# Zero matmuls ahead of the first data, a first product in written order, a two-instruction root step and larger stores in a two-layer decoder trunk

## The chip, the cores and the metric

The kernel runs on one core of a Trainium2 chip. The metric is device time in microseconds, from the first to the last of the program as the device counts it; the median of three runs is 2240.84 (2240.35 to 2241.23). The profile is one execution, taken apart from those runs.

## What is computed

A trunk of two layers on 256 tokens of 2048 features, all in float32. Each layer adds a mixer and then a squared-ReLU MLP to the residual x, each behind an RMS norm, and a last RMS norm ends it:

```python
for layer in range(DEPTH):
    j = layer // 2
    h = rmsnorm(x, ln_mix[layer])
    if layer % 2 == 0:
        x = x + even_mixer(h, e_w_in[j], e_g_q[j], e_g_kv[j], e_w_uq[j], e_w_ukv[j], e_w_out[j], rope128, rope64)
    else:
        x = x + odd_mixer(h, o_w_in[j], o_w_out[j], rope128)
    h = rmsnorm(x, ln_mlp[layer])
    x = x + squared_relu_mlp(h, mlp_w1[layer], mlp_w2[layer])
return rmsnorm(x, ln_final)
```

Only two places of this matter here: the first 512 columns of `h @ e_w_in` (the queries' latent of the even mixer), and the last norm.

## The kernel before

**Tiles.** 256 tokens are two tiles of 128 (t = 0, 1), 2048 features are sixteen blocks of 128 (k = 0 to 15). Every operand of a large product is split into a high and a low half (`xh`, `xl` for the activations, both in the tile `xx`; `wh`, `wl` for the weights), so that one product is three matmuls: high by high (L170), high by low (L171), low by high (L172). Weights come from memory into one of three `raw` buffers by the queue of SP (L150); ACT makes the high half (a cast, L162), DVE subtracts it for the low half (L163).

**The first product.** `even_mixer` (L500) starts with `TokenGemm` on 512 columns of the weights: sixteen rows of weights, six matmuls of 512 columns for each. `step(i)` does rows 2i and 2i+1, `rows` any number. The activations are made on the way: `scaled_transpose` (L260) turns two blocks of features on PE (four transposes into one PSUM tile `pt`, L236), then for each block ACT copies it times its gain into `xh` (L270) and DVE makes `xl` (L271). `norm_block(..., late=True)` gives these as parts [0] and [1] and, as part [2], the squares of both tiles of tokens over 512 columns on ACT (`sumsq`, L258). The gains themselves are rows of 128 that are loaded and turned on PE (`load_gains`, L488): `pg` of 32 columns for ln_mix, later one of 38 for ln_mlp, e_g_q and e_g_kv.

**What sets the order.** The kernel is written in the order of its data; the framework's scheduler then reorders each engine's instructions by its own estimate, here too, and places the waits. On the chip every engine takes its own list in the order in which it stands. The queue of SP issues x in blocks of columns (`load_x`, L97), the identity (`cst`, L100), the rows of gains (L494) and the weights.

**The end.** The last MLP's `down` does its last 256 columns one tile of tokens after the other and calls `leave(t, cs)` (L809) for each: the sum of squares of the last columns (L813), `inverse_root` (L245: a guess from the exponent's bits at L249 and L250, then three Newton steps of three DVE instructions, L252 to L254), five pieces of the row scaled by the root on DVE and ACT in turn (L817 to L821), and four stores of 512 columns on SP's queue (L823).

Of the kernel before, what the change touches and what calls it, by code (L numbers as in the profile page):

```python
# [12 lines left out]
F32 = mybir.dt.float32  # L13
# [7 lines left out]
P = 128  # L21
# [19 lines left out]
def shape_constants():  # L41
    """Identity, rotary tables, and additive masks: functions of the shapes alone. Row p is token p of
    either tile, in cosT and sinT feature p; the first tile's queries see 128 keys, the second's 256."""

    def rope(dim):
        inv = (10000.0 ** (-np.arange(0, dim, 2, dtype=np.float32) / np.float32(dim)).astype(np.float64)).astype(np.float32)
        ang = (np.arange(S, dtype=np.float32)[:, None] * inv[None, :]).astype(np.float64)
        c, s = np.cos(ang).astype(np.float32), np.sin(ang).astype(np.float32)
        return c, s

    q = np.arange(S)[:, None]
    k = np.arange(S)[None, :]
# [15 lines left out]
def decoder_trunk(ctx, tc, const, x_in, ln_mix, ln_mlp, ln_final, e_w_in, e_g_q, e_g_kv, e_w_uq, e_w_ukv, e_w_out,  # L68
# [29 lines left out]

    load_x(0, 256)
    nc.sync.dma_start(ident, const[:, :P])  # L100
    # the activation table is loaded while the first data is on its way
    warm = small.tile([P, 1], F32, name="warm")
    nc.vector.memset(warm, 0.0)
    nc.scalar.activation(warm, warm, AF.Exp)

# [13 lines left out]
    # Slots whose readers may still be pending: taking one runs what frees it.  # L119
# [12 lines left out]
    class Weights:  # L132
        """Rows of 128 of the columns in srcs: four at a time (or as in loads) from memory, two at a time split."""
# [10 lines left out]
        def load(self):  # L144
            at, n = self.loads.popleft()
            raw = self.flat("raw", F32, n, 3, 2048)
            c = 0
            for s in self.srcs:
                w = s.shape[-1]
                nc.sync.dma_start(raw[:, :, c : c + w], s[at * P : (at + n) * P, :].rearrange("(k p) n -> p k n", p=P))  # L150
                c += w
            self.raw.append((at, n, raw))
# [23 lines left out]
    def bank(shape=(P, 512), wide=False):  # L176
        """A bank to accumulate in; wide: the scores' banks too."""
        if wide and next(turns) % 6 >= 4:
            return psc.tile(list(shape), F32, name=nm("acc"), tag="ps")
        return acc.tile(list(shape), F32, name=nm("acc"), tag="acc")  # L180

    class TokenGemm:
        """Tokens on partitions: o[t] is [P, width] for each tile of tokens. srcs: weights' columns."""
# [11 lines left out]
        def rows(self, k0, n):  # L195
            ah, al = self.act
            wh, wl = self.w.get(k0, n)
# [41 lines left out]
    def rsqrt(y, ss, n, mean_over):  # L239
        """y = (ss / mean_over + EPS) ** -0.5 on [P, n]."""  # L240
# [4 lines left out]
    def inverse_root(y, v, n):  # L245
        """v ** -0.5: a guess from the exponent's bits, Newton steps."""
# [13 lines left out]
    def scaled_transpose(src, gain, dst_h, dst_l):  # L260
        """dst[f, k, tok] = src[tok, k, f] * gain[f, k], in halves; src(t, k) is [P tokens, P features]. A list of parts."""
# [14 lines left out]
    def norm_block(i, n, ss, late=False):  # L276
        """Columns of the residual that are final: x.T * gain, as parts, and their part of the sum of squares."""
# [22 lines left out]
    def rope(dst, src, nh, hd, t, r):  # L300
        """dst, src: [P, nh * hd]; src times the row's r, rotated."""
# [29 lines left out]
    def heads(pool, src, tab, rate=1):  # L331
        """Four heads of 128 features of x, rotated, features on partitions: [P, 4, S]."""
# [24 lines left out]
    def attend(pool, scores, bias, scale, values, oh, ol, o0, done):  # L357
        """scores(h, out, t) fills [P, keys]; values(h, t): [P, HD]. Head h goes to oh/ol[:, o0 + h, :]."""
# [51 lines left out]
    def plain_transpose(tok, dst, done=None):  # L410
        """tok: a tile of rows for each tile of tokens; dst(k0, n, PSUM) stores n tiles of features. A list of parts."""
# [18 lines left out]
    def rotated(pool, o, hd, r, width=512):  # L430
        """Rotates [P, width] of both tiles of tokens."""
# [7 lines left out]
    def split_rows(pool, o, hd, r):  # L439
        """Rotates [P, 512] of both tiles and, later, puts features on partitions: [P, 4, S] in halves."""  # L440
# [24 lines left out]
    def project_out(oT, w, ss, i):  # L465
        """The first two blocks of columns begin while the last heads are pending."""
# [21 lines left out]
    def load_gains(at, gs):  # L488
        """Gains by feature: rows of 128, turned on the tensor engine."""
# [9 lines left out]

    def even_mixer(ss):  # L500
        w = e_w_in[0]
        with ExitStack() as st:
# [5 lines left out]
            # queries' and keys' latents, with the first norm on the way  # L508
            g = TokenGemm(act, KT, [w[:, 0:512]], loads=[(0, 1), (1, 1), (2, 2)] + [(k, 4) for k in range(4, KT, 4)])
            parts = [norm_block(0, n, ss, True) for n in range(4)]  # L510
            g.w.load()
            load_gains(0, [ln_mix])
            load_x(256, 512)
            parts[0][0]()
            g.rows(0, 1)
            g.w.load()
            parts[0][1]()
            g.rows(1, 1)
            load_x(512, 1024)
            g.w.load()  # L520
            parts[1][0]()
            g.step(1)
            parts[1][1]()
            load_x(1024, 1536)
            g.step(2)
            parts[0][2]()
            parts[2][0]()
            g.step(3)
            parts[2][1]()
            load_x(1536, 2048)  # L530
            g.step(4)
            parts[3][0]()
            load_gains(2 * KT, [ln_mlp, e_g_q, e_g_kv])
            nc.sync.dma_start(cst[:, P:], const[:, P:])
            g.step(5)
            parts[3][1]()
            for n in range(1, 4):
                parts[n][2]()
            g.step(6)
            g.step(7)  # L540
# [17 lines left out]
            # c_kv, k_pe, k_idx, w_idx; the two single keys padded for either head of a pair  # L558
# [24 lines left out]
            # index scores and the keys that they choose, as parts  # L583
# [135 lines left out]
    def mlp(layer, ss, done, tail=None):  # L719
        w1, w2 = mlp_w1[layer], mlp_w2[layer]  # L720
        NCH = 4
        with ExitStack() as st:
# [6 lines left out]
            def up(c):  # L729
                """Hidden features on partitions: relu(x @ w1) ** 2, transposed, of 2048 features."""  # L730
# [19 lines left out]
            def down(c, h):  # L750
# [10 lines left out]
                if last and tail:  # L761
                    # the last columns: one tile of tokens after the other, so that the first ends under the second
# [38 lines left out]
    def both(n, cs):  # L801
# [3 lines left out]
        if n == 3:  # L805
            nc.vector.tensor_reduce(pre, ss3, axis=AX.X, op=ALU.add)
            nc.vector.tensor_scalar(pre, pre, 1.0 / D, EPS, op0=ALU.mult, op1=ALU.add)

    def leave(t, cs):  # L809
# [3 lines left out]
        nc.vector.tensor_tensor_reduce(junk[:, : cs.stop - cs.start], x[:, t, cs], x[:, t, cs], 1.0 / D, pre[:, t : t + 1],  # L813
                                       op0=ALU.mult, op1=ALU.add, accum_out=v)
        inverse_root(r, v, 1)
        xt = x[:, t, :]
        nc.vector.tensor_scalar_mul(xt[:, :512], xt[:, :512], r)  # L817
        nc.scalar.activation(xt[:, 512:1024], xt[:, 512:1024], AF.Copy, scale=r)
# [3 lines left out]
        for h in range(0, D, 512):  # L822
            nc.sync.dma_start(ov[t][:, h : h + 512], xt[:, h : h + 512])  # L823
# [29 lines left out]
```

## Time and profile before

| | |
|---|---|
| median of the runs | 2240.84 us |
| span of the profiled execution | 2239.9 us |
| PE busy | 2224.8 us, 99% of the span |
| DVE busy | 1318.0 us, 59% |
| ACT busy | 1036.4 us, 46% |
| moved by DMA | 406.65 MB, mean 182 GB/s |

The span runs from the first to the last instruction of the profiled execution, and it is the time that sums are made against; the median of the runs lies 0.9 us above it. PE's busy time is made of overlapping pieces: a matmul's row ends with its last result, and the next has begun before that, so the pace of a row of matmuls is the distance of their starts, not the length of one. In the chain of waits that overlap is already taken off.

### The profile page before, as it was taken

How to read it: one execution, taken by the hardware profiler on the slowest of the kernel's cores; microseconds unless marked ns; L12 is line 12 of the kernel's file. 1: busy time of each engine (PE TensorE's matmuls, PEld its weight loads, DVE VectorE, ACT ScalarE, POOL GpSimd, SP SyncE). 2: the span in 40 equal slices, each digit the busy share in tenths (PEclk: the TensorE clock that was granted, in tenths of full speed). 3: DMA queues.
4: the chain of work that ended last, by engine and by line, in shares of the span. 5: the costliest groups of instructions: out<-in, count | busy, mean ns of one | idle time of the engine just before them, and what ended most of it. 6: DMA issues, size and time to landing. Idle time of an engine off the chain costs nothing.

```text
span 2239.9 us, 29663 instructions
## 1 busy us (share of the span) xinstructions
PE 2224.8 (99%) x12126; PEld 1913.7 (85%) x12126; DVE 1318.0 (59%) x1771; ACT 1036.4 (46%) x1369; POOL 0.2 (0%) x4
## 2 busy tenths in 40 slices
PE   8999999999999999999999999999999999999998
PEld 7899988888888888888899999888888888888887
DVE  6767665565545545655575666556565555465555
ACT  5444545555434434534444443455454344344333
POOL 0000000000000000000000000000000000000000
PEclk9999999999999999999999999999999999999999
DMA  7554545555555555555555555556555555555553
GB/s 244 177 164 148 170 137 172 183 187 187 188 188 189 188 188 190 188 188 186 188 171 170 177 164 170 173 180 204 190 181 192 189 191 188 188 187 190 188 188 132
DMA packets 207605, 406.65 MB, mean 182 GB/s; under 512 B 8614, under 2 KB 15468, under 8 KB 207340
## 3 DMA queue, kind: packets, MB, share of 16 engines
q1 hardware_dynamic: 207468, 404.75, 55.5%
q8 instruction: 95, 1.56, 0.3%
q14 instruction: 42, 0.34, 0.0%
HBM read 402.62 MB, written 2.10 MB: 181 GB/s over the span
## 4 chain that ended last, share of the span: by engine, by line
PE 99%; DMA 0%; DVE 0%; ACT 0%; SPq 0%; issue 0%; DVEq 0%
PE acc L226 21%; PE acc L172 21%; PE acc L171 21%; PE acc L170 21%; PE acc L227 11%; PE pt L236 1%; PE ps L458 1%; PE po L391 1%; PE pp L236 0%; PE po L392 0%; DMA raw<-in_e_w_in_dram 0%; PE ps L689 0%; PE ps L688 0%; DMA raw<-in_mlp_w_dram 0%; PE pi L170 0%; PE pi L171 0%
## 5 line engine op out<-in xcount | busy, mean ns | idle before, releaser
L163 DVE TENSOR_TENSOR wl<-raw,wh 128x1024 fp32r<-128x1024 f32 (+3 forms) x765 | 927.6, 1213 | 849.0 <-ACT wh L162 843.1
L162 ACT CAST wh<-raw 128x1024 fp32r<-128x1024 f32 (+3 forms) x765 | 794.5, 1039 | 1081.3 <-PE acc L172 572.1
L226 PE MATMUL acc<-xx,wh 128*128 128x512 f32 x2048 | 703.6, 395 | 0.0
L227 PE MATMUL acc<-xx,wl 128*128 128x256 f32 x2048 | 544.1, 281 | 0.0
L226 PEld LDWEIGHTS acc<-xx,wh 128*128 128x128 f32 x2048 | 378.2, 188 | 77.9
L172 PE MATMUL acc<-wh,hl 128*128 128x512 f32 (+1 forms) x1024 | 402.2, 393 | 0.0
L171 PE MATMUL acc<-wl,hh 128*128 128x512 f32 (+1 forms) x1024 | 400.0, 391 | 0.0
L227 PEld LDWEIGHTS acc<-xx,wl 128*128 128x128 f32 x2048 | 385.5, 188 | 12.5
L170 PE MATMUL acc<-wh,hh 128*128 128x512 f32 (+1 forms) x1024 | 361.0, 391 | 0.0
L171 PEld LDWEIGHTS acc<-wl,hh 128*128 128x128 f32 x1024 | 192.2, 188 | 45.8
L170 PEld LDWEIGHTS acc<-wh,hh 128*128 128x128 f32 x1024 | 191.7, 188 | 45.2
L172 PEld LDWEIGHTS acc<-wh,hl 128*128 128x128 f32 x1024 | 192.3, 188 | 44.2
L171 PE MATMUL acc<-xx,wh 128*128 128x256 f32 x768 | 216.5, 282 | 0.0
L170 PE MATMUL acc<-xx,wh 128*128 128x256 f32 x768 | 216.4, 282 | 0.0
L172 PE MATMUL acc<-xx,wl 128*128 128x256 f32 x768 | 215.5, 282 | 0.0
L171 PEld LDWEIGHTS acc<-xx,wh 128*128 128x128 f32 x768 | 144.7, 188 | 0.4
L170 PEld LDWEIGHTS acc<-xx,wh 128*128 128x128 f32 x768 | 144.7, 188 | 0.4
L172 PEld LDWEIGHTS acc<-xx,wl 128*128 128x128 f32 x768 | 144.3, 188 | 0.0
L171 PE MATMUL acc<-wl,xx 128*128 128x512 f32 (+1 forms) x320 | 127.5, 399 | 0.0
L172 PE MATMUL acc<-wh,xx 128*128 128x512 f32 (+1 forms) x320 | 125.5, 393 | 0.0
L170 PE MATMUL acc<-wh,xx 128*128 128x512 f32 (+1 forms) x320 | 119.7, 400 | 0.5 <-ACT xx L270 0.5
L171 PE MATMUL acc<-wl,oh 128*128 128x512 f32 x256 | 102.2, 399 | 0.0
(166 smaller groups left out, 1615.8 us busy)
## 6 DMA issues: line engine op xcount, KB each, us to landing
raw<-in_mlp_w_dram SPq DMA_DIRECT2D x252, 1024.0 KB, 5.1
raw<-in_o_w_in_dram SPq DMA_DIRECT2D x48, 1024.0 KB, 5.1
raw<-in_e_w_in_dram SPq DMA_DIRECT2D x35, 1024.0 KB, 5.1
raw<-in_e_w_out_dram SPq DMA_DIRECT2D x16, 1024.0 KB, 5.0
raw<-in_o_w_out_dram SPq DMA_DIRECT2D x16, 1024.0 KB, 5.1
raw<-in_mlp_w_dram SPq DMA_DIRECT2D x8, 512.0 KB, 3.8
raw<-in_e_w_uq_dram SPq DMA_DIRECT2D x4, 768.0 KB, 4.4
raw<-in_e_w_in_dram SPq DMA_DIRECT2D x4, 640.0 KB, 4.1
```

Of the source, the lines that this page charges most:

```text
L162: nc.scalar.copy(hi, raw)
L163: nc.vector.tensor_tensor(lo, raw, hi.bitcast(F32), op=ALU.subtract)
L170: nc.tensor.matmul(o, ah, bh, start=first, stop=False, **kw)
L171: nc.tensor.matmul(o, ah, bl, start=False, stop=False, **kw)
L172: nc.tensor.matmul(o, al, bh, start=False, stop=last, **kw)
L226: nc.tensor.matmul(self.o[f], wh[:, kk, fs], xx[:, k], start=k == 0, stop=False, skip_group_check=True)
L227: nc.tensor.matmul(self.o[f][:, 0, :], wl[:, kk, fs], xx[:, k, 0], start=False, stop=k == KT - 1, skip_group_check=True)
L236: nc.tensor.transpose(o, src, ident[: src.shape[0], : src.shape[0]])
L391: nc.tensor.matmul(po[0][:, h % 2, :], values(h, 0), pr[h][:, :S], start=True, stop=False)
L458: nc.tensor.matmul(o, q[:, h, t * P : t * P + P], k[:, h, : SPAN[t][1]], start=True, stop=True)
```

## The change

Four things are changed.

- **Ahead of the data.** A tile of zeros is set on DVE, and PE does seven matmuls of 512 columns on it before anything else. The identity and the rows of ln_mix (now a tile of their own, `rows0`) are loaded through ACT's queue.
- **The first product.** It moves into a new function, `first_product`, in a block in which the scheduler keeps the written order. The loads of x and weights stand together at its beginning; the first four rows of weights share one buffer and come in four loads; rows 0 to 3 are multiplied one at a time; the high half of row 0 is made on DVE. The loads of the second group of gains and of the remaining constants are issued after it.
- **The root.** `leave` no longer calls `inverse_root`; it halves its argument and does a Newton step in two DVE instructions instead of three.
- **The stores.** Each tile of tokens leaves in two stores of 1024 columns; the last one of the second tile is issued by ACT.

```diff
     load_x(0, 256)
-    nc.sync.dma_start(ident, const[:, :P])
+    nc.scalar.dma_start(ident, const[:, :P])
+    rows0 = cpool.tile([2 * KT, P], F32, name="rows0")
+    nc.scalar.dma_start(rows0, ln_mix.rearrange("l (k p) -> (l k) p", p=P))
+    zeros = wpool.tile([P, 512], F32R, name="zeros", tag="ra", bufs=1)
+    nc.vector.memset(zeros.bitcast(F32), 0.0)
     warm = small.tile([P, 1], F32, name="warm")
...
+    pw = psc.tile([P, 512], F32, name="pw", tag="ps")
+    for i in range(7):
+        nc.tensor.matmul(pw, zeros[:, :P], zeros, start=True, stop=True)
...
+    def first_product(g, w, parts):
+        raw = g.w.load(((0, 1), (1, 1)))
+        load_x(256, 512)
+        g.w.load(((2, 1), (3, 1)), raw)
+        load_x(512, 1024)
+        g.w.load(((4, 2), (6, 2)))
+        load_x(1024, 1536)
+        g.w.load(((8, 4),))
+        load_x(1536, 2048)
+        pg = psc.tile([P, 512], F32, name="pg", tag="ps")
+        pt = ptr.tile([P, 2, S], F32, name="pt0", tag="pt")
+        transposed(pg[:, : 2 * KT], rows0)
...
+        for a, b, k0 in ((xh, wh, True), (xl, wh, False), (xh, wl, False)):
+            for t in range(NT):
+                nc.tensor.matmul(g.o[t], a[:, 0, t * P : t * P + P], b, start=k0, stop=False)
+        parts[0][1]()
+        g.product(1, 1, *wts[1])
+        g.rows(2, 1)
+        parts[1][0]()
+        g.rows(3, 1)
+        parts[1][1]()
+        parts[0][2]()
+        g.step(2)
+        g.w.load(((12, 4),))
+        parts[2][0]()
+        parts[1][2]()
+        g.step(3)
+        parts[2][1]()
+        g.step(4)
+        parts[3][0]()
+        parts[2][2]()
+        g.step(5)
+        parts[3][1]()
+        parts[3][2]()
+        g.step(6)
+        g.step(7)
...
+            g = TokenGemm(act, KT, [w[:, 0:512]])
             parts = [norm_block(0, n, ss, True) for n in range(4)]
+            with tc.manual_schedule():
+                first_product(g, w, parts)
             load_gains(2 * KT, [ln_mlp, e_g_q, e_g_kv])
             nc.sync.dma_start(cst[:, P:], const[:, P:])
...
-        inverse_root(r, v, 1)
+        for _ in range(3):
+            nc.vector.scalar_tensor_tensor(b.bitcast(F32), r, v, r, op0=ALU.mult, op1=ALU.mult)
+            nc.vector.scalar_tensor_tensor(r, b.bitcast(F32), 1.5, r, op0=ALU.subtract, op1=ALU.mult)
         xt = x[:, t, :]
-        nc.vector.tensor_scalar_mul(xt[:, :512], xt[:, :512], r)
-        nc.scalar.activation(xt[:, 512:1024], xt[:, 512:1024], AF.Copy, scale=r)
+        nc.scalar.activation(xt[:, :512], xt[:, :512], AF.Copy, scale=r)
+        nc.vector.tensor_scalar_mul(xt[:, 512:1024], xt[:, 512:1024], r)
+        nc.sync.dma_start(ov[t][:, :1024], xt[:, :1024])
...
-        for h in range(0, D, 512):
-            nc.sync.dma_start(ov[t][:, h : h + 512], xt[:, h : h + 512])
+        (nc.scalar if t else nc.sync).dma_start(ov[t][:, 1024:], xt[:, 1024:])
```

What the block of written order makes of the engines' lists is not in these lines, so the place that decides follows, on two engines. A row is the line, the operation, what it writes and reads with buffer numbers, and the shape.

ACT before, in the middle of the first product. `wh_150` is the high half of rows 2 and 3, `wh_178` of 4 and 5, `wh_207` of 6 and 7; `pt_141` and `pt_166` hold the transposed features 4 to 7; `junk` rows are squares.

```order
L162 CAST wh_150<-raw_139 128x1024
L258 ACTIVATE junk_297,ss_82<-x 128x512
L270 ACTIVATE xx<-pt_141,gains 128x256
L270 ACTIVATE xx<-pt_166,gains 128x256
L258 ACTIVATE junk_299,ss_82<-x 128x512
L270 ACTIVATE xx<-pt_141,gains 128x256
L270 ACTIVATE xx<-pt_166,gains 128x256
L162 CAST wh_178<-raw_176 128x1024
L162 CAST wh_207<-raw_176 128x1024
L258 ACTIVATE junk_301,ss_82<-x 128x512
```

ACT after, about the same place. `wh_178` is now row 3, `wh_201` rows 4 and 5, `wh_232` rows 6 and 7; `pt_169` holds features 4 and 5, `pt_188` 6 and 7, `pt_219` 8 and 9.

```order
L284 ACTIVATE xx<-pt_169,gains 128x256 x2
L174 CAST wh_178<-raw_104 128x512
L284 ACTIVATE xx<-pt_188,gains 128x256 x2
L272 ACTIVATE junk_197,ss_94<-x 128x512
L272 ACTIVATE junk_199,ss_94<-x 128x512
L174 CAST wh_201<-raw_111 128x1024
L284 ACTIVATE xx<-pt_219,gains 128x256 x2
L272 ACTIVATE junk_228,ss_94<-x 128x512
L272 ACTIVATE junk_230,ss_94<-x 128x512
L174 CAST wh_232<-raw_111 128x1024
```

The casts, which stood two in a row, now stand singly, each behind two copies out of a fresh `pt` tile and, from `wh_201` on, two squares (but for one).

PE before, the transposes of features 4 to 7 and the first matmuls on rows 2 and 3.

```order
L236 MATMUL pt_141<-cst,x 128x128 x4
L236 MATMUL pt_166<-cst,x 128x128 x4
L170 MATMUL acc_88<-wh_150,xx 128x512
L170 MATMUL acc_89<-wh_150,xx 128x512
L171 MATMUL acc_88<-wl_151,xx 128x512
L172 MATMUL acc_88<-wh_150,xx 128x512
L171 MATMUL acc_89<-wl_151,xx 128x512
```

PE after, from the transposes of features 4 and 5 to the first matmuls on rows 4 and 5. `pg_352` is the turn of the second group of gains.

```order
L250 MATMUL pt_169<-cst,x 128x128 x4
L250 MATMUL pg_352<-cst,rows_348 128x38
L182 MATMUL acc_100<-wh_178,xx 128x512
L183 MATMUL acc_100<-wl_179,xx 128x512
L184 MATMUL acc_100<-wh_178,xx 128x512
L182 MATMUL acc_101<-wh_178,xx 128x512
L183 MATMUL acc_101<-wl_179,xx 128x512
L184 MATMUL acc_101<-wh_178,xx 128x512
L250 MATMUL pt_188<-cst,x 128x128 x4
L182 MATMUL acc_100<-wh_201,xx 128x512
L183 MATMUL acc_100<-wl_202,xx 128x512
```

Two blocks were turned in one go ahead of two steps; now one block is turned ahead of each step, and the turn of the gains stands ahead of row 3. The same alternation of four transposes and one step goes on to step 6.

## Rows read from the trace of the kernel before

**Rows 1.** The page: the chain that ended last, by engine.
```profile
PE 99%; DMA 0%; DVE 0%; ACT 0%; SPq 0%; issue 0%; DVEq 0%
```

**Rows 2.** Stretches: length, busy time per engine, PEclk, DMA share, GB/s.
```profile
0.00:15.00 15.00, 9.33 (x29) 7.03 (x30) 4.55 (x9) 8.95 (x20) 0.20 (x4) 1.00 0.83 275
15.00:37.00 22.00, 22.00 (x103) 17.53 (x102) 16.43 (x37) 13.93 (x26) 0.00 (x0) 1.00 0.74 251
...
100.00:2215.00 2115.00, 2115.00 (x11564) 1819.52 (x11563) 1236.17 (x1580) 975.64 (x1266) 0.00 (x0) 1.00 0.55 180
```

**Rows 3.** Waits of PE, 0 to 50 us: total, times, longest.
```profile
PE pt L236 <- DMA cst<-in_const_dram: 3.9, 1, 3.9
PE pt L236 <- DMA x<-in_x_dram: 1.2, 1, 1.2
PE acc L170 <- ACT xx L270: 0.5, 1, 0.5
```

**Rows 4.** Chain of waits, 12 to 26 us: start, us, what.
```profile
12.82 0.85 PE acc L172 x2
...
20.62 0.23 PE acc L170
...
25.00 1.02 PE pt L236 x8
```

**Rows 5.** Timeline of ACT: start, us, what, [idle before and what ended it].
```profile
6.60 0.63 ACT L258 ACTIVATE junk<-x 128x512 f32<-128x512 f32 x1 [0.52 <-DMA x<-in_x_dram]
...
9.09 0.62 ACT L162 CAST wh<-raw 128x512 fp32r<-128x512 f32 x1 [1.77 <-DMA raw<-in_e_w_in_dram]
9.62 0.63 ACT L258 ACTIVATE junk<-x 128x512 f32<-128x512 f32 x1
...
10.95 0.62 ACT L258 ACTIVATE junk<-x 128x512 f32<-128x512 f32 x1
...
11.70 0.63 ACT L258 ACTIVATE junk<-x 128x512 f32<-128x512 f32 x1
...
12.33 0.45 ACT L270 ACTIVATE xx<-pt,gains 128x256 fp32r<-128x256 f32 x1
12.68 1.03 ACT L162 CAST wh<-raw 128x1024 fp32r<-128x1024 f32 x1
...
16.34 0.83 ACT L270 ACTIVATE xx<-pt,gains 128x256 fp32r<-128x256 f32 x2
```

**Rows 6.** Timeline of DVE, same columns.
```profile
13.75 1.23 DVE L163 TENSOR_TENSOR wl<-raw,wh 128x1024 fp32r<-128x1024 f32 x1 [0.45 <-ACT wh L162]
15.07 0.48 DVE L271 SCALAR_TENSOR_TENSOR xx<-pt,gains,xx 128x256 fp32r<-128x256 f32 x1
```

**Rows 7.** Timeline of PE, same columns.
```profile
3.94 1.09 PE L236 MATMUL pt<-cst,x 128*128 128x128 f32 x4 [3.94 <-DMA cst<-in_const_dram]
...
10.75 0.79 PE L170 MATMUL acc<-wh,xx 128*128 128x512 f32 x1 [0.51 <-ACT xx L270]
...
37.06 0.53 PE L170 MATMUL acc<-wh,xx 128*128 128x400 f32 x2
```

**Rows 8.** DMA issues, 0 to 22 us: count, KB each, us to landing.
```profile
rows<-in_ln_mlp_dram SPq DMA_DIRECT2D x1, 16.0 KB, 9.8
```

**Rows 9.** Timelines of PE, DVE and ACT at the end.
```profile
2230.36 0.28 PE L172 MATMUL acc<-hh,hl 128*128 128x256 f32 x1
...
2229.58 0.16 DVE L254 SCALAR_TENSOR_TENSOR r<-t,r 128x1 f32<-128x1 f32 x1
2229.77 0.49 DVE L817 TENSOR_SCALAR x<-x,r 128x512 f32<-128x512 f32 x1
...
2230.97 0.48 DVE L748 SCALAR_TENSOR_TENSOR x<-acc,rr,x 128x256 f32<-128x256 f32 x1
...
2234.13 0.72 ACT L818 ACTIVATE x<-x,r 128x512 f32<-128x512 f32 x1 [3.24 <-DVE r L254]
```

**Rows 10.** Stretches at the end, columns as in rows 2.
```profile
2230.00:2233.00 3.00, 0.64 (x6) 0.43 (x4) 2.76 (x12) 0.89 (x2) 0.00 (x0) 1.00 0.63 234
...
2234.00:2235.00 1.00, 0.00 (x0) 0.00 (x0) 0.96 (x4) 0.87 (x2) 0.00 (x0) 0.50 0.00 0
```

More of the change, by code (lines that the diff above doesn't have):

```diff
@@ L142, in flat, with load @@
             return t[:, : n * self.width].rearrange("p (k n) -> p k n", n=self.width)
[L144 to L152, printed above, removed]
+        def load(self, pieces=None, raw=None):
+            if raw is None:
+                at, n = self.loads.popleft()
+                raw = self.flat("raw", F32, n, 3, 2048)
+                self.raw.append((at, n, raw))
+            first = self.raw[-1][0]
+            for at, n in pieces or (self.raw[-1][:2],):
+                c = 0
+                for s in self.srcs:
+                    w = s.shape[-1]
+                    nc.sync.dma_start(raw[:, at - first : at - first + n, c : c + w], s[at * P : (at + n) * P, :].rearrange("(k p) n -> p k n", p=P))
+                    c += w
+            return raw
         def get(self, k, n, into=None):
@@ L195, in rows, with product @@
         def rows(self, k0, n):
+            self.product(k0, n, *self.w.get(k0, n))
+        def product(self, k0, n, wh, wl):
             ah, al = self.act
-            wh, wl = self.w.get(k0, n)
             for kk in range(n):
@@ L498, in load_gains @@
         nc.vector.tensor_copy(gains[:, at : at + n], pg[:, :n])
+    def first_product(g, w, parts):
[10 more added lines that the diff above has]
+        transposed(pg[:, : 2 * KT], rows0)
+        for j in range(2):
+            for t in range(NT):
+                transposed(pt[:, j, t * P : t * P + P], x[:, t, j * P : j * P + P])
+        nc.vector.tensor_copy(gains[:, : 2 * KT], pg[:, : 2 * KT])
+        raw = g.w.raw[0][2]
+        wts = [[g.w.flat(h, F32R, 1, 3, 1024) for h in ("wh", "wl")] for _ in range(2)]
+        nc.vector.tensor_copy(wts[0][0], raw[:, 0:1])
+        for k in range(2):
+            nc.scalar.activation(xh[:, k, :], pt[:, k, :], AF.Copy, scale=gains[:, k : k + 1])
+            nc.vector.scalar_tensor_tensor(xl[:, k, :], pt[:, k, :], gains[:, k : k + 1], xh[:, k, :].bitcast(F32), op0=ALU.mult, op1=ALU.subtract)
+            if k:
+                nc.scalar.copy(wts[k][0], raw[:, k : k + 1])
+            nc.vector.tensor_tensor(wts[k][1], raw[:, k : k + 1], wts[k][0].bitcast(F32), op=ALU.subtract)
+        wh, wl = (h[:, 0, :] for h in wts[0])
+        for a, b, k0 in ((xh, wh, True), (xl, wh, False), (xh, wl, False)):
+            for t in range(NT):
+                nc.tensor.matmul(g.o[t], a[:, 0, t * P : t * P + P], b, start=k0, stop=False)
[20 more added lines that the diff above has]
+        g.step(7)
     def even_mixer(ss):
@@ L506, in even_mixer @@
             act = (xh, xl)
-            g = TokenGemm(act, KT, [w[:, 0:512]], loads=[(0, 1), (1, 1), (2, 2)] + [(k, 4) for k in range(4, KT, 4)])
+            g = TokenGemm(act, KT, [w[:, 0:512]])
             parts = [norm_block(0, n, ss, True) for n in range(4)]
[L511 to L532, printed above, removed]
+            with tc.manual_schedule():
+                first_product(g, w, parts)
             load_gains(2 * KT, [ln_mlp, e_g_q, e_g_kv])
             nc.sync.dma_start(cst[:, P:], const[:, P:])
[L535 to L540, printed above, removed]
             r = finish_norm(ss)
@@ L806, in both @@
             nc.vector.tensor_reduce(pre, ss3, axis=AX.X, op=ALU.add)
-            nc.vector.tensor_scalar(pre, pre, 1.0 / D, EPS, op0=ALU.mult, op1=ALU.add)
+            nc.vector.tensor_scalar(pre, pre, 0.5 / D, 0.5 * EPS, op0=ALU.mult, op1=ALU.add)
     def leave(t, cs):
@@ L812, in leave @@
         junk = wpool.tile([P, 512], F32, name=nm("junk"), tag="junk", bufs=1)
-        nc.vector.tensor_tensor_reduce(junk[:, : cs.stop - cs.start], x[:, t, cs], x[:, t, cs], 1.0 / D, pre[:, t : t + 1],
+        nc.vector.tensor_tensor_reduce(junk[:, : cs.stop - cs.start], x[:, t, cs], x[:, t, cs], 0.5 / D, pre[:, t : t + 1],
                                        op0=ALU.mult, op1=ALU.add, accum_out=v)
-        inverse_root(r, v, 1)
+        b = small.tile([P, 1], I32, name=nm("b"))
+        nc.vector.tensor_scalar(b, v.bitcast(I32), 1, None, op0=ALU.logical_shift_right)
+        nc.vector.tensor_scalar(r.bitcast(I32), b, -1.0, 1597463007.0 - 2.0**22 - 2.0**31, op0=ALU.mult, op1=ALU.add)
+        for _ in range(3):
+            nc.vector.scalar_tensor_tensor(b.bitcast(F32), r, v, r, op0=ALU.mult, op1=ALU.mult)
+            nc.vector.scalar_tensor_tensor(r, b.bitcast(F32), 1.5, r, op0=ALU.subtract, op1=ALU.mult)
         xt = x[:, t, :]
-        nc.vector.tensor_scalar_mul(xt[:, :512], xt[:, :512], r)
-        nc.scalar.activation(xt[:, 512:1024], xt[:, 512:1024], AF.Copy, scale=r)
+        nc.scalar.activation(xt[:, :512], xt[:, :512], AF.Copy, scale=r)
+        nc.vector.tensor_scalar_mul(xt[:, 512:1024], xt[:, 512:1024], r)
+        nc.sync.dma_start(ov[t][:, :1024], xt[:, :1024])
         nc.vector.tensor_scalar_mul(xt[:, 1024:1536], xt[:, 1024:1536], r)
```

## The prediction, made before the changed kernel was run

> **What bounds the kernel now.** I read the page first: the chain of work that ended last is 99% PE [rows 1]. So only two places can give time: the start, before PE runs without gaps, and the end, after its last matmul. The table of stretches says where the start ends: PE is busy 9.33 of the first 15 us, then all of 15 to 37 us and all of 100 to 2215 us [rows 2]. The waits of PE in the first 50 us are three: 3.9 for the first data, 1.2 for the second block of x, 0.5 for ACT [rows 3]. Beside them stands a slow pace: at 12.8 us two matmuls of 512 columns take 0.85, so 0.43 each, and at 20.6 one takes 0.23 [rows 4]. The granted clock's row reads 1.00 in both stretches [rows 2], but a pace of half the later one is the 1.2 GHz level, so I go by the pace. The first product is over at 37.06, where the first matmuls of 400 columns start [rows 7]. At the end, the last matmul stops at 2230.64 and the second tile's work begins on DVE at 2230.97 [rows 9].
>
> One thing more is to be seen in 15 to 37 us: ACT (13.93) and DVE (16.43) work beside a full PE [rows 2]. That is the cover the change touches.
>
> **The change part by part.** *Zeros.* Seven matmuls of 512 columns at 0.43 take 3.0 us, from about 1.3 (an estimate: a memset goes ahead of them) to 4.3, under the 3.9 of waiting. At most they push the first transposes by 0.4. If they bring the upper clock early, the twelve matmuls before 13.5 give back 12 x 0.2 = 2.4 and the sixteen slow transposes about 1.4 (1.09 for four against half of 1.02 [rows 4, 7]); this is part of where the steps begin, below.
>
> *Loads.* Identity and ln_mix go to ACT's queue, ahead of its table load, when ACT has no data to work on; nobody waits. SP's first weights are issued about 0.5 earlier. One late load matters: the gains' rows (ln_mlp, e_g_q, e_g_kv) are issued behind all of x and twelve rows of weights, and PE turns them (pg_352) before it may do the fourth row. The ln_mlp load took 9.8 us to land under traffic [rows 8]; issued at 9 to 10 us, the rows land at about 18.
>
> *The fixed order.* This is the term that decides. In the order of before, ACT casts rows 4 to 7 back to back (wh_178, wh_207), and the transposes of two blocks stand together. In the new order ACT's row is: two copies out of pt_188, two squares, cast wh_201; and PE's row is: the matmuls on wh_178, the transposes into pt_188, the matmuls on wh_201. Every step up to the sixth is written so. ACT takes its queue in order: at 9.09 it had stood 1.77 behind a cast whose weights were late, and the square behind that cast ran only at 9.62, though the other half of its block of x had been squared at 6.60 [rows 5]. So the cast for a step cannot start until PE has finished the step before and turned the next block. Cast, squares, copies and matmuls, which overlapped, now stand in series.
>
> The series for one step (two rows of weights, twelve matmuls), from its last transpose: copy on ACT 0.45, its low half on DVE 0.48, a second copy 0.36 to 0.38 more (0.83 for two), two squares 0.75 and 0.63, cast 1.03, and six handovers of 0.04 (cast end 13.71 to DVE's start 13.75): 3.93 [rows 5, 6]. Then PE does one matmul and waits for the low half of the weights, 1.23 on DVE after the cast: 5.2 from the last transpose [rows 6]. Eleven matmuls of 0.23 and four transposes (half of 1.02, with 0.2 until the last result is out) follow: 2.56 + 0.7. Sum 8.5 at the upper clock; at the lower 5.2 + 4.7 + 1.09 = 11.0 [rows 4, 7]. Before, the same work took 2.8 + 0.5 = 3.3. Without squares (step 4) it is 7.1 or 9.6; step 6 has no transposes behind it, 7.8 or 9.9; step 7 finds its cast done, 2.8 or, half at either clock, 3.5. Steps 2 to 7: 3 x 8.5 + 7.1 + 7.8 + 2.8 = 43.2, or 33.0 + 9.6 + 9.9 + 3.5 = 56.0.
>
> Which clock? Each gap leaves PE one matmul in 5.2 us. At the end of the kernel the granted clock is down to 0.50 from 2234 on, 3.4 us after the last matmul [rows 9, 10]. At the start PE ran without a gap from 10.75 [rows 7], had two slow matmuls at 12.82, and the upper pace in the matmuls that follow the next transposes. A slow step keeps PE busy for 4.7 + 1.09 = 5.8 us at a stretch, so the clock can come up late in a step and go down in the next gap. I take half of the steps at either clock: 49.6.
>
> The second copy waits for DVE, in the order of before as in the new one; no two copies of one block stand next to each other in the trace. If it need not wait, each series is 0.55 shorter, 2.7 in five steps, and the time 2271. The Trainium skill, page "PSUM — Partial Sum Buffer", section "PSUM bank collisions raise a hardware error", has the accesses of two engines to one bank kept apart, reads too. By it the longer series stands; the trace has no row that could show it.
>
> *Where the steps begin.* First data near 4.2, matmuls of the first row at 5.9, six of them to 8.4, transposes to 9.4; then the same series with a cast half as wide and no squares (about 2.1, and 0.75 for the low half) to 12.2; five matmuls and transposes to 14.1 or 15.4; the series again, and the gains' rows at 18, to 18.7; five matmuls, transposes: 20.6 or 21.6. I take 21.0; 18.3 if the rows are early. Product over at 21.0 + 49.6 = 70.6 against 37.06: **33.5 late**. PE had no idle time left from there to the end [rows 1, 2], so nothing gives it back.
>
> *Root and stores.* Six small DVE steps instead of nine, 0.19 apart [rows 9]: 0.58 less per tile. In the first tile only 0.3 counts, since PE's last matmul ends at 2230.64 and the second tile's add started at 2230.97. The second root is then ready 0.9 earlier. The first store now waits for ACT's copy, 0.72, instead of DVE's, 0.49 [rows 9], so it is issued 0.25 later after the root; the bytes behind it are the same. Gain 0.65; bounds 0, if larger pieces end that much later, and 1.0.
>
> *Sum.* On the profiled execution 2239.9 + 33.5 - 0.65 = 2272.8. The median 2240.84 lies 0.9 above that span, so 2273.7, which I give as **2273.5**.
>
> **The rivals.** *All steps at the lower clock.* For it: every gap is about as long as the one in which the clock went down at the end. Against: PE is busy for 5.8 us at a stretch in a slow step. 21.6 + 56.0 - 37.06 - 0.65 = 39.9: 2280.7. The Trainium skill, page "TensorE: Matmul & The Clock Gate", section "Why this matters for your kernels", warns that idle gaps between bursts of matmuls bring the lower clock back. By that rule this rival holds; the trace has only the fall at the end for it.
>
> *Faster: the order does not bind, the zeros pay.* If ACT's and DVE's work stays under PE's matmuls as it did from 15 to 37 us, the start gives back PE's 1.2 + 0.5 of waits and 2.4 + 1.4 of slow pace, and the end 0.65: 6.1, so 2234.7, between 2232 and 2240 as the clock comes early or not. It decides if the casts are ready when PE has turned a block, that is if the 5.2 of a gap shrinks below about 1. For it: ACT has the room, 13.93 of 22 us [rows 2]. Against: the two orders, and ACT standing in order at 9.09 [rows 5].
>
> *The zeros don't raise the clock.* Then 1 us more at the start (21.6 and 22 for 21.0); inside the range.
>
> **How the numbers follow.** Forecast (about half of the steps slow) 0.70, all slow 0.20, order harmless 0.10. Low end: 18.3 - 1 + 43.2 - 2.7 = 57.8, so 20.7 late and 1.0 won: 2260.5; high end 22 + 56 = 78, nothing won at the end: 2281.8. With 1 to 2 us for the durations of one execution: 2258 to 2283. A measurement of this kernel tells 0.2% (4.5 us) from no change. Slower by more 0.90; the harmless case straddles the line, 0.05 within and 0.05 faster.
>
> **What would show it.** Right: between 20 and 70 us PE has five waits of 2.5 to 4 us that ACT ends and five of about 1 us that DVE's low half ends, each behind a cast that starts after the transposes; a granted clock of 0.50 somewhere there; the first 400-column matmul near 70; pg_352 waiting for a DMA near 18; six root rows of 0.16, and a span after the last matmul shorter by 0.5 to 0.9. Wrong: casts that start while the matmuls of the step before run, PE full from 20 us on, or a product that ends before 45.

## The result, and the profile after

The changed kernel takes **2278.04 us** (2277.59 to 2279.91, five runs) against 2240.63 for the kernel before in the same runs: a ratio of 1.0168, 95% interval 1.0157 to 1.0179. It is 37.4 us slower. The forecast was 2273.5, the range 2258 to 2283.

The profiled execution took 2277.59 with a span of 2275.7, which is 35.8 longer than the span of before (to the hundredth, the traces hold 2275.73 and 2239.86). First the page's chain by engine, beside [rows 1]:

```profile
PE 98%; DMA 1%; ACT 1%; DVE 1%; issue 0%; SPq 0%; DVEq 0%
```

PE still sets the end, but no longer without a gap. The table of stretches (length, busy time of PE, PEld, DVE, ACT, POOL with counts, granted clock, DMA share, GB/s), beside [rows 2]:

```profile
0.00:15.00 15.00, 12.06 (x38) 8.37 (x38) 4.88 (x11) 4.40 (x8) 0.20 (x4) 1.00 0.86 305
15.00:37.00 22.00, 9.84 (x31) 6.82 (x31) 6.24 (x10) 7.88 (x17) 0.00 (x0) 0.78 0.33 118
37.00:72.00 35.00, 23.30 (x61) 16.66 (x60) 10.92 (x26) 10.12 (x20) 0.00 (x0) 0.65 0.24 71
100.00:2215.00 2115.00, 2115.00 (x11543) 1817.35 (x11542) 1241.06 (x1604) 976.47 (x1262) 0.00 (x0) 1.00 0.55 181
```

PE was busy all of 15 to 37 us and is now busy 9.84 of 22. From 100 us on PE is full in both. So the loss lies between 15 and 75 us. The waits of PE up to 85 us (total, times, longest), beside [rows 3]:

```profile
PE acc L182 <- ACT wh L174: 18.8, 6, 3.9
PE pg L250 <- DMA rows<-in_ln_mlp_dram: 3.5, 1, 3.5
PE acc L183 <- DVE wl L175: 2.6, 6, 0.5
PE pw L111 <- DVE warm L107: 1.4, 1, 1.4
PE acc L545 <- ACT xx L537: 0.6, 1, 0.6
```

Before it waited for data and, once, 0.5 for ACT. Now 18.8 us are waits for a cast (`wh`) and 2.6 for its low half (`wl`). PE's timeline, cut to the start of each step and the end of the product (start, duration, what, [idle time before and what ended it]), beside [rows 7]:

```profile
18.46 0.22 PE L250 MATMUL pg<-cst,rows 38*128 38x38 f32 x1 [3.46 <-DMA rows<-in_ln_mlp_dram]
...
20.12 0.60 PE L250 MATMUL pt<-cst,x 128*128 128x128 f32 x4
24.60 0.79 PE L182 MATMUL acc<-wh,xx 128*128 128x512 f32 x1 [3.89 <-ACT wh L174]
25.86 0.79 PE L183 MATMUL acc<-wl,xx 128*128 128x512 f32 x1 [0.47 <-DVE wl L175]
26.45 0.63 PE L184 MATMUL acc<-wh,xx 128*128 128x512 f32 x1
...
30.64 0.60 PE L250 MATMUL pt<-cst,x 128*128 128x128 f32 x4
35.13 0.80 PE L182 MATMUL acc<-wh,xx 128*128 128x512 f32 x1 [3.89 <-ACT wh L174]
...
74.87 0.34 PE L183 MATMUL acc<-wl,xx 128*128 128x400 f32 x1
```

The further steps start at 44.16 (a gap of 2.52), 55.13 and 65.75 (3.89 each). Two matmuls of 400 columns stand ahead of 74.87 among those of 512, 0.36 in all, so the product is over at 74.5, where it was over at 37.06. In the second gap, ACT and then DVE (same columns), beside [rows 5, 6]:

```profile
20.75 0.47 ACT L284 ACTIVATE xx<-pt,gains 128x256 fp32r<-128x256 f32 x1 [3.71 <-PE pt L250]
21.78 0.47 ACT L284 ACTIVATE xx<-pt,gains 128x256 fp32r<-128x256 f32 x1 [0.55 <-DVE xx L285]
22.15 0.62 ACT L272 ACTIVATE junk<-x 128x512 f32<-128x512 f32 x1
...
22.89 0.63 ACT L272 ACTIVATE junk<-x 128x512 f32<-128x512 f32 x1
...
23.52 1.03 ACT L174 CAST wh<-raw 128x1024 fp32r<-128x1024 f32 x1
```

```profile
21.26 0.48 DVE L285 SCALAR_TENSOR_TENSOR xx<-pt,gains,xx 128x256 fp32r<-128x256 f32 x1 [2.35 <-ACT xx L284]
...
24.58 1.23 DVE L175 TENSOR_TENSOR wl<-raw,wh 128x1024 fp32r<-128x1024 f32 x1 [1.81 <-ACT wh L174]
```

ACT stood still for 3.71 us until PE had turned the block at 20.12. Only then do copy, copy, two squares and the cast follow, and PE does nothing until 24.60. The weights that the cast reads were issued at 4.34 and took 7.4 us to land, so they had been there all that time; only the place of the cast in ACT's queue held it.

The granted clock, in stretches cut where it changes, the first from the transposes on (columns as above):

```profile
20.12:23.70 3.58, 0.59 (x5) 0.35 (x3) 0.97 (x2) 2.36 (x7) 0.00 (x0) 1.00 0.56 216
23.71:30.53 6.82, 5.46 (x12) 3.98 (x13) 1.23 (x1) 0.84 (x1) 0.00 (x0) 0.50 0.00 0
30.53:33.94 3.41, 0.71 (x5) 0.36 (x3) 0.97 (x2) 2.08 (x5) 0.00 (x0) 1.00 0.00 0
33.95:40.77 6.82, 5.18 (x11) 3.76 (x12) 1.23 (x1) 1.13 (x3) 0.00 (x0) 0.50 0.40 120
40.77:44.18 3.41, 0.89 (x7) 0.52 (x5) 1.01 (x3) 1.88 (x3) 0.00 (x0) 1.00 0.00 0
```

The upper level (1.00, 2.4 GHz) is granted in stretches in which PE works 0.59 to 0.89 us, the lower one (0.50, 1.2 GHz) in those that hold a step's twelve matmuls. It comes up as a step ends and is spent on the next gap. This goes on to 71.5.

At the end of the kernel: PE's last matmul, then DVE, beside [rows 9].

```profile
2266.97 0.28 PE L184 MATMUL acc<-hh,hl 128*128 128x256 f32 x1
```

```profile
2267.29 0.48 DVE L790 SCALAR_TENSOR_TENSOR x<-acc,rr,x 128x256 f32<-128x256 f32 x1
...
2268.71 0.22 DVE L862 SCALAR_TENSOR_TENSOR b<-r,v 128x1 f32<-128x1 f32 x1
2268.97 0.16 DVE L863 SCALAR_TENSOR_TENSOR r<-b,r 128x1 f32<-128x1 f32 x1
...
2270.06 0.49 DVE L866 TENSOR_SCALAR x<-x,r 128x512 f32<-128x512 f32 x1
```

From the last matmul's end to the end of the span it is 2275.73 - 2267.25 = 8.48, where it was 2239.86 - 2230.64 = 9.22: 0.74 won.

### The profile page after: what moved, and what is told of

It is laid out like the page before. It is cut to its first block, busy times and chain, and to the rows that moved or that the text cites. A ratio compares the mean times of both kernels' runs of the same rounds, so it can differ in the third digit from the quotient of the medians.

```text
span 2275.7 us, 29668 instructions
## 1 busy us (share of the span) xinstructions
PE 2240.4 (98%) x12133; PEld 1921.6 (84%) x12133; DVE 1320.3 (58%) x1768; ACT 1037.2 (46%) x1369; POOL 0.2 (0%) x4
## 4 chain that ended last, share of the span: by engine, by line
PE 98%; DMA 1%; ACT 1%; DVE 1%; issue 0%; SPq 0%; DVEq 0%
PE acc L183 21%; PE acc L240 21%; PE acc L184 21%; PE acc L182 21%; PE acc L241 11%; PE pt L250 1%; PE ps L472 1%; PE po L405 1%; PE pp L250 0%; DMA rows<-in_ln_mlp_dram 0%; PE po L406 0%; DVE wl L175 0%; ACT junk L272 0%; PE ps L731 0%; PE ps L730 0%; DMA x<-in_x_dram 0%
## 5 line engine op out<-in xcount | busy, mean ns | idle before, releaser
L241 PEld LDWEIGHTS acc<-xx,wl 128*128 128x128 f32 x2048 | 385.4, 188 | 12.5
L182 PE MATMUL acc<-wh,xx 128*128 128x512 f32 (+1 forms) x318 | 124.7, 414 | 18.8 <-ACT wh L174 18.8
L184 PE MATMUL acc<-wh,xx 128*128 128x512 f32 (+1 forms) x318 | 128.2, 403 | 0.0
```

Source lines behind the costliest of these rows:

```text
L241: nc.tensor.matmul(self.o[f][:, 0, :], wl[:, kk, fs], xx[:, k, 0], start=False, stop=k == KT - 1, skip_group_check=True)
```

## The experiments

**The same instructions in the scheduler's own order.** Everything else of the change stays.

```diff
-            with tc.manual_schedule():
-                first_product(g, w, parts)
+            first_product(g, w, parts)
```

> The changed kernel with the block of written order taken away, all else as changed, so the scheduler orders the first product again. Theory A (the written order puts cast, squares, copies and matmuls in series): the five gaps of 2.5 to 3.9 us go, PE is full from about 18 us, the first product ends at 33 to 38 us, time 2235 to 2241. Theory B (the loss is in the loads in pieces, the ACT queue or the zeros): time stays above 2260.

Measured: 2240.68 (ten runs), ratio 0.9999, interval 0.999 to 1.0009. The written order is the whole loss. But in this order the zeros and the shorter end win nothing either. PE's waits up to 85 us, then two lines of ACT's timeline:

```profile
PE acc L545 <- ACT xx L537: 1.8, 1, 1.8
PE pw L111 <- DVE warm L107: 1.4, 1, 1.4
PE pt L250 <- DMA x<-in_x_dram: 0.6, 1, 0.6
```

```profile
7.31 0.63 ACT L272 ACTIVATE junk<-x 128x512 f32<-128x512 f32 x1
...
8.45 0.46 ACT L537 ACTIVATE xx<-pt,gains 128x256 fp32r<-128x256 f32 x1
```

This order puts squares and a cast ahead of the first copy out of `pt`, so PE's first product stands for 1.8 us, and in this execution the granted clock, up before, was down at 0.50 again from 9.25 to 12.66. That these two eat what the other parts give is likely, not shown. For the first row the written order is the better one (0.6); for the steps it is the worse one.

**The written order with the casts one step earlier.** The weights of a step are cast and split one step earlier, ahead of the copies and squares that stood in front of them. The transposes of each block move one step earlier too, and some squares move behind. All else of the change stays. A piece of the edit:

```diff
         parts[1][0]()
-        g.rows(3, 1)
+        g.product(2, 1, *cur)
+        cur, nxt = nxt, g.w.get(4, 2)
         parts[1][1]()
+        g.product(3, 1, *cur)
+        cur, nxt = nxt, g.w.get(6, 2)
         parts[0][2]()
-        g.step(2)
+        parts[2][0]()
+        g.product(4, 2, *cur)
```

> The changed kernel, still in written order, but each step's cast and low half are written one step earlier, ahead of the transposes of the next block. Theory A (the cast behind the copies is what PE waits for): gaps of under 0.5 us, the granted clock stays at 1.00 from its first rise on, the product ends at 36 to 41 us, time 2235 to 2242. Theory B (transposes one block at a time, or the loads, are what costs): more than half of the loss stays, over 2258.

Measured: 2238.2 (2237.79 to 2240.36, ten runs), ratio 0.999, interval 0.9981 to 0.9999. PE's waits up to 85 us, then ACT's casts:

```profile
PE pw L111 <- DVE warm L107: 1.4, 1, 1.4
PE acc L183 <- DVE wl L175: 0.8, 2, 0.7
PE acc L545 <- ACT xx L537: 0.6, 1, 0.6
PE pg L250 <- DMA rows<-in_ln_mix_dram: 0.5, 1, 0.5
```

```profile
14.99 1.04 ACT L174 CAST wh<-raw 128x1024 fp32r<-128x1024 f32 x1
15.93 0.48 ACT L284 ACTIVATE xx<-pt,gains 128x256 fp32r<-128x256 f32 x1
...
18.09 1.04 ACT L174 CAST wh<-raw 128x1024 fp32r<-128x1024 f32 x1
```

The casts run back to back with the copies, no step waits for one, and the clock stays up: 21.4 us of waits for casts and low halves have shrunk to 0.8. A written order does no harm as such; one in which the casts stand behind copies that wait for PE does. Whether the earlier casts or the earlier transposes alone would do, no run separates. This version has the lowest median of the study, 0.1% under the kernel before.

**The squares behind the cast.** In each full step the two squares are written behind the product's call instead of ahead of it (first of four such moves):

```diff
         parts[1][1]()
+        g.step(2)
         parts[0][2]()
-        g.step(2)
         g.w.load(((12, 4),))
```

> The changed kernel with each pair of squares written behind the step's cast instead of ahead of it. Theory A (all of ACT's work between the transposes and the cast is in series): the four gaps of 3.9 become 2.5 as in step 4, 4 x 1.38 = 5.5 off if the clock stays low in every step, 2272.5; up to 10 off if the shorter gaps keep the clock up in half of the steps. Theory B (the squares were covered): 2278 within 1.

Measured: 2271.83 (four runs), ratio 1.0138, interval 1.0123 to 1.0153, 6.2 less than the changed kernel. Every gap is now 2.52 where four of five were 3.89, so the squares are in the series for the 1.38 that was put down for them. Four times 1.37 is 5.5 of the 6.2; the rest can be the clock, which was up for part of more steps than before. Two of the steps, from one start to the next:

```profile
24.57:33.17 8.60, 5.31 (x16) 3.86 (x17) 2.20 (x4) 3.23 (x8) 0.00 (x0) 0.78 0.00 0
33.17:42.55 9.38, 6.39 (x16) 4.48 (x16) 2.19 (x4) 3.17 (x7) 0.00 (x0) 0.66 0.31 87
```

**Twelve matmuls into a spare bank in each gap.** They add work and change no result.

```diff
+        def keep():
+            for _ in range(12):
+                nc.tensor.matmul(pw.rearrange("p (a b) -> p a b", a=2), xh[:, 0, :P], xx[:, 0], start=True, stop=True)
...
+        keep()
         g.step(2)
```

> The changed kernel with twelve matmuls of 512 columns on data that is there, into a bank that nobody reads, between the four transposes and each of the steps 2 to 6; the chain of the casts stays. Theory A (a step costs 10.5 instead of 8.5 because the granted clock falls in its gap): the clock stays at 1.00, steps take 8.4 and 7.0, time 2278 - 10 = 2268, with 2266 to 2270. Theory B (the slow pace of the steps is not the gap's doing): fillers at 0.43 take 5.1 us in a gap of 3.9, each step gets 1.2 longer, 2283 or more.

Measured: 2271.59 (four runs), ratio 1.0133, interval 1.0116 to 1.015. More work by sixty matmuls, and 6.5 less time. The steps, from one start to the next:

```profile
26.05:34.48 8.43, 6.54 (x28) 4.82 (x28) 2.19 (x4) 3.22 (x7) 0.00 (x0) 1.00 0.01 2
34.48:41.54 7.06, 6.30 (x28) 4.82 (x29) 2.19 (x4) 1.89 (x3) 0.00 (x0) 1.00 0.40 116
...
49.96:59.92 9.96, 8.07 (x29) 6.00 (x29) 3.00 (x9) 3.28 (x8) 0.00 (x0) 0.83 0.29 82
```

At the upper clock a full step takes 8.43. The one without squares takes 7.13: its row ends at 41.54, but the next first matmul starts at 41.61, behind the last filler. The changed kernel's steps took 10.5 to 11.0 and 9.0. The 1.9 to 2.5 between them are the clock's share of a step. The run is over its expectation because the clock fell in the wait for the second gains, which has no filler, and stayed down into the first gap, and because it fell again in the fourth of these steps and in the one behind it (0.50 from 61.44 to 64.86).

**The end alone.** The kernel before with the new root, the scaling of the first columns on ACT and two stores a tile:

```diff
-        inverse_root(r, v, 1)
+        for _ in range(3):
+            nc.vector.scalar_tensor_tensor(b.bitcast(F32), r, v, r, op0=ALU.mult, op1=ALU.mult)
+            nc.vector.scalar_tensor_tensor(r, b.bitcast(F32), 1.5, r, op0=ALU.subtract, op1=ALU.mult)
...
-        for h in range(0, D, 512):
-            nc.sync.dma_start(ov[t][:, h : h + 512], xt[:, h : h + 512])
+        (nc.scalar if t else nc.sync).dma_start(ov[t][:, 1024:], xt[:, 1024:])
```

> The kernel before with only the end of the change: the shorter root, the first 512 columns scaled on ACT, two stores a token tile, the very last one issued by ACT. Theory A (the span after the last matmul is shorter by the 0.81 us that the changed kernel showed, 9.26 to 8.45, and nothing in front of it moves): 2239.8 against 2240.6. Theory B (the run under the scheduler's own order had the same shorter end and was no faster, so something takes it back): 2240.6, the end being shorter only from the last matmul on. Under either, root rows of 0.22 and 0.16 us in turn, six of them 1.35 in all.

Measured: 2239.93 (eleven runs) against 2240.95, ratio 0.9995, interval 0.9986 to 1.0004. The 1.0 agrees with the changed kernel's trace (0.74; the expectation's 0.81 comes from spans rounded to 0.1) and with the run's own, which ends 8.31 after the last matmul, 0.91 sooner than before. The interval does not tell it from nothing. The trace shows something else: the start is the kernel before's, yet the product is over sooner.

```profile
36.09 0.52 PE L170 MATMUL acc<-wh,xx 128*128 128x400 f32 x2
```

It was 37.06 in the profiled execution of before [rows 7]. There matmuls went at 0.43 each until 13.5, and the eight transposes behind them, from 13.47, took 1.85 where the next eight took 1.03; here matmuls go at 0.23 from 10.5 on. In the traces the upper level is on record from 15.1 us there and from 9.8 here. So the same start got the upper clock some 5 us sooner in one execution than in another, worth about 1 us: two waits that were not there before, 0.93 and 0.49, took part of it back.

**No zeros.** The version with the casts ahead, without the memset and the seven matmuls.

```diff
-    zeros = wpool.tile([P, 512], F32R, name="zeros", tag="ra", bufs=1)
-    nc.vector.memset(zeros.bitcast(F32), 0.0)
...
-    for i in range(7):
-        nc.tensor.matmul(pw, zeros[:, :P], zeros, start=True, stop=True)
```

> The kernel with the casts one step ahead, without the seven matmuls on zeros and their memset. Theory A (the zeros only fill the wait for the first data; the clock's rise does not hang on them): 2238.2 as with them, PE's first wait back to about 4 us. [...]

Measured: 2239.67 (2239.22 to 2240.22, eleven runs), 1.5 more than with them, and 1.3 more than the version with a start without pauses below, which ran on the same chip and none of whose runs took over 2238.51. The zeros are worth something, under half of the 3.8 that the prediction allowed them. How they win it the traces don't show: matmuls reached the upper pace at 11.4 us without the zeros and at 12.5 with them, in an execution that was the slowest of its ten.

**The second gains early.** The changed kernel, with the three loads issued by ACT's queue at the start.

```diff
+    rows1 = wpool.tile([P, P], F32, name="rows1", tag="ra", bufs=1)
+    n = 0
+    for g in (ln_mlp, e_g_q, e_g_kv):
+        g = g.rearrange("l (k p) -> (l k) p", p=P)
+        nc.scalar.dma_start(rows1[n : n + g.shape[0], :], g)
+        n += g.shape[0]
```

> The changed kernel with its written order, and the rows of the second gains (ln_mlp, e_g_q, e_g_kv) loaded by ACT's queue at the start, behind identity and ln_mix; the zeros stand in an unused part of xx for it. Prediction's term: the steps begin at 18.3 instead of 21.0 with early rows, so 2.7 less, 2275.3. Rival: behind the wait of 3.46 us stands a cast that ends at 17.05 and a low half that ends at 17.77, so only about 1.15 comes back and a wait on ACT of about 2 us takes its place: 2276.9. If the clock also comes up in another step because of it, some 2 us more in either direction.

Measured: 2275.98 (four runs), ratio 1.0158, interval 1.0144 to 1.0172, 2.1 less than the changed kernel. PE's timeline around the place of the wait:

```profile
13.15 0.60 PE L256 MATMUL pt<-cst,x 128*128 128x128 f32 x4
15.85 0.49 PE L188 MATMUL acc<-wh,xx 128*128 128x512 f32 x1 [2.10 <-ACT wh L180]
...
17.84 0.60 PE L256 MATMUL pt<-cst,x 128*128 128x128 f32 x4
```

The steps begin 2.28 sooner (17.84 against 20.12). But 1.25 of that is there already at the transposes ahead of the wait (13.15 against 14.40): the clock came up sooner in this execution. The wait of 3.46 for the rows gave way to one of 2.10 for the cast, as the rival said, and in this pair of profiles the rows themselves are worth about 1.0. The time does not decide: 2275.98 lies 0.7 from the prediction's 2275.3 and 0.9 from the rival's 2276.9.

**A start without pauses.** The version with the casts ahead, with eight matmuls on zeros and two more behind the first transposes.

```diff
-    for i in range(7):
+    for i in range(8):
...
+        for i in range(2):
+            nc.tensor.matmul(pw, zeros[:, :P], zeros, start=True, stop=True)
```

> The kernel with the casts one step ahead, with eight matmuls on zeros ahead of the first data and two more behind the first transposes, where PE waits 0.56 us for ACT. Theory A (the clock rises after a stretch without idle time; PE is then busy from 1.4 us on): upper clock before 9.2 us instead of 12.54, some eight matmuls of 512 columns 0.2 us shorter each, product over at about 36 and 2236.5 to 2237. Theory B (when it rises does not hang on these gaps of half a microsecond): clock as before and the added matmuls cost up to 0.5: 2238.2 to 2238.8.

Measured: 2238.33 (2238.10 to 2238.51, eleven runs), ratio 0.9989, interval 0.998 to 0.9997. The profiled execution had the upper pace by 8 us and its product over at 35.31, against 37.32 with the casts ahead alone. The medians, 2238.33 and 2238.2, don't differ: that profiled execution of the other version had taken 2240.36, its slowest. What differs is the spread, 0.4 us against 2.6, on two different chips. That a start without pauses makes the rise of the clock regular would explain it; it is argued from two profiles, not shown.

**The order alone.** The changed kernel without zeros and with the end of before (these parts as in the diffs above, taken back).

> The changed kernel without the matmuls on zeros and with the root, the scaling and the four 512-column stores of before: the written order and its loads alone. If the parts add up, that is the changed kernel's 2278.0 plus 1.0 (the end alone) plus 1.4 (the zeros under the order with casts ahead): 2280.4. Rival: the wait for the second gains' rows, over at 18.5 whatever the first matmuls do, swallows what the zeros win, so the zeros are worth nothing here: 2279.0. The steps of 9 to 11 us behind 20 us are the same under both.

Measured: 2279.65 (2277.81 to 2280.57, four runs), ratio 1.0172, interval 1.0156 to 1.0189. It lies between the two expected times and decides neither, for the wait that was to swallow the gain was gone: without the zeros the turn of the second gains moved behind the next transposes. Its steps are those of the changed kernel; the first, from its start to the next:

```profile
23.42:34.32 10.90, 6.55 (x17) 4.62 (x17) 2.19 (x4) 3.21 (x7) 0.00 (x0) 0.66 0.00 0
```

**Filled gaps and early gains together**, the edits of both runs above.

> The changed kernel with twelve matmuls into a spare bank in each gap (as in the run before that did so) and the second gains' rows early (as in the run before that did so), so that no long wait stands on PE before the steps. Theory A (the clock falls only where PE has a gap): the upper clock from 10 us at the latest to the end, every full step about 8.4 us, the prediction's 8.5, in place of 10.5 to 11, and the wait's 2: 2278.0 - 2 - 5 x 2.2 = 2265. Theory B (it falls now and then whatever PE does, as twice in the run with filled gaps): one or two steps at the lower clock, 2269 to 2270.

Measured: 2270.7 (2269.01 to 2272.26, four runs), ratio 1.0133, interval 1.0115 to 1.0151. The first and the third of four steps took 8.43 and 8.37 at the upper clock. The rows of the other two (the third step begins at 41.29, so the second took 8.67):

```profile
32.62:41.22 8.60, 7.84 (x28) 5.95 (x28) 2.19 (x4) 1.89 (x3) 0.00 (x0) 0.80 0.33 95
...
49.66:59.61 9.95, 8.03 (x28) 5.96 (x28) 2.98 (x9) 3.27 (x8) 0.00 (x0) 0.83 0.29 82
```

Theory A falls. With waits of about 1.1 and 0.76 left in a step, the clock still fell in two of these four and in the step behind them, and the second step took 8.67 where 7.13 is to be had. Which pauses bring it down, and when, these runs leave open.

## Why the prediction was right, and where it was off

**The mechanism is the one forecast.** Five waits of PE for a cast, 2.52 to 3.89 each (forecast 2.5 to 4), the cast started behind transposes, copies and squares; then five for its low half, 0.47 (forecast about 1: the slower matmul ahead of each covers the rest); the wait for the second gains' rows up to 18.46; the product over at 74.5 (forecast 70.6). Taking back the order takes back all of the loss, and so does keeping a written order with casts and transposes one step ahead.

**The series.** From the last transpose (20.72) to the first matmul of the step 3.88, forecast 3.93; to the second matmul 5.14, forecast 5.2. The second copy does wait for DVE, 0.55 on the path each time, as the longer sum had it. For the dependency, the Trainium skill, page "PSUM — Partial Sum Buffer", section "PSUM bank collisions raise a hardware error", was cited, by which the accesses of two engines to one bank are kept apart; the trace agrees in that the wait is there (0.55 behind DVE's low half). That the chip would need it no run here shows.

**The steps.** From one first matmul to the next, with the matmuls at the lower clock, 10.97, 10.53 and 10.62 us and 9.03 without squares, forecast 11.0 and 9.6; at the upper clock, which only the filled gaps gave, 8.43 and 7.13, forecast 8.5 and 7.1. The seventh step took 2.8, forecast 2.8 or 3.5; by the prediction's own paces half of it at either clock is 4.0, an error of 0.25 in the 49.6.

**The clock's share is the term that was mis-sized.** The prediction took half of the steps at either clock, because a slow step keeps PE busy for 5.8 us and the clock "can come up late in a step". It did come up late: at 30.53, with the last transposes, when there was nothing left to speed up. The upper level held for a third of the time and fell on the gaps. From the steps' begin the product took 74.5 - 20.7 = 53.8 where 49.6 were forecast, 4.2 more. Of the steps only the seventh, with nothing to wait for, had the upper clock, and the transposes had it in part. The mistake was to halve the steps: a level granted for part of the time helps only by the work that lies in that part. The rival with all steps at the lower clock had this right, and its 2280.7 lies nearer than 2273.5. The rule named with it, of the Trainium skill, page "TensorE: Matmul & The Clock Gate", section "Why this matters for your kernels", that idle gaps between bursts of matmuls bring the lower clock back, agrees with the trace: 0.50 in each stretch that holds a step.

**Where the steps begin.** 20.7, forecast 21.0. That early rows would give 18.3 counted 2.7 for them; in the pair of profiles they gave about 1.0 by themselves, since the cast behind them was not ready sooner, while the medians differ by 2.1.

**The end.** 0.74, forecast 0.65, but by other sizes. The root's rows were put at 0.16 each and 0.19 apart; those on line 862 take 0.22 and the next starts 0.26 later, so the six take 1.35 where nine took 1.75, and 0.40 is won, not 0.58. The 0.29 at the start of the second tile came as forecast: its add begins at 2267.29, right behind PE's last matmul. The rest, 0.05, lies behind the root, in the scaling and the stores, which were put at a loss of 0.25.

**The zeros.** 1.3 to 1.5 where no later wait takes it, of the 3.8 allowed if they brought the upper clock early. In the changed kernel they end at 4.8, and the matmuls went at the upper pace from 10.1 on; the kernel with the order alone, without zeros, had it from 9.7 on. So neither in this pair of profiles nor in that of the versions with the casts ahead did the seven matmuls bring the upper clock earlier, and where their gain comes from stays open.

**The sum.** Forecast span 2272.8; -0.3 for the steps' begin, +4.2 for the clock, -0.1 for the end make 2276.6, and the span is 2275.7. The missing 0.8 lies between the product's end and the last matmul: 2230.64 - 37.06 = 2193.58 before, 2267.25 - 74.5 = 2192.75 after. About 0.65 of it is lost by the kernel before between 2206 and 2217 us, in a stretch that neither the change nor the prediction is about: its matmuls of 256 columns start 0.120 apart there, the changed kernel's 0.117, and two of them, at 2215.70, take 0.54 until the next one starts, the changed kernel's 0.23. The cause stays open. Another 1.6 lies outside the span: the prediction went 0.7 above it, the result is 2.3 above, of which 0.45 is that the profiled execution was the quickest of five. Every execution whose span is on record took 1.73 to 1.91 more than its span, whatever the kernel. If the profiled execution of before did too, it took about 2241.7, some 0.9 more than the median of its runs; the late rise of its clock can be the reason.

## What to carry to other kernels

An engine takes its queue in order, so an order written by hand must put what needs only loaded data (here a cast of weights) ahead of what waits for the engine it feeds; here the place of the casts, with the transposes and squares around them, decided 40 us. Where PE waits in every step of a loop as long as here (2.5 to 3.9 us behind the transposes), price the step at the lower clock in full, since the upper level may come up just when the work is over and be spent on the next wait. And where a profiled execution is the base of a sum, compare it with the median of its kernel first, since the start alone made about 1 us of difference between two executions of the same code.

## What was not expected of the hardware

- The granted clock fell into step with the loop: 6.82 us at 0.50 and 3.41 at 1.00 in turn, from 23.71 to 71.5, with 5.2 to 5.5 us of work in the former in the stretches shown and 0.6 to 0.9 in the latter. The kernel with the order alone shows the same.
- Sixty matmuls more made the kernel 6.5 us faster.
- Of two small DVE instructions of one kind on 128x1, the one with a column as its scalar (L862) took 0.22, the one with a constant (L863) 0.16, so six rows of a shorter root do not save a third of nine.
